# Adding the expert sums into the residual: products with gate 2 before the last expert's values, and the residual store on another queue

## The chip, the cores and the metric

The kernel runs on one core of a Trainium2 chip. The metric is the device time of one execution in microseconds (us). A core has five engines that run side by side, each from its own queue in order: TensorE (PE in the profile, PEld its weight loads), VectorE (DVE), ScalarE (ACT), GpSimd (POOL) and SyncE (SP, which here only issues DMAs). Matrix products land in PSUM; VectorE and ScalarE read it, GpSimd does not.

## The reference

Two layers work on 256 tokens `x` and 256 context tokens `xc`, each 1024 wide, in float32. In each layer:

```
mod        = silu(c) @ w_ada + b_ada          # six parts of 1024: ..., gt2
x          = x + gt1 * (mixers(norm(x), norm(xc)) @ w_out)
x          = x + gt2 * moe(norm(x))           # 16 experts, 2 of them per token
xc         = the same with its own gates, in the first layer only
```

`moe` sums, per token, gate times expert output. The final output is `rms_norm(x)` times a gain. The change touches only how `x + gt2 * moe` (and `xc + gtc2 * moe`) is put together, and what follows it.

## The kernel before, in words

**Experts.** `moe` runs 16 steps one after the other. Each step gathers the rows of one expert, multiplies them by w1, w3 and w2 (six weight blocks of 1 MB, loaded by SP), and adds its rows, scaled by the routing gate, to a table `ybd` in device memory by an accumulating DMA from GpSimd (`add_rows`). The first layer has four row tiles of 128 (two of context, two of tokens), the second has two.

**The last step.** Step 15 does not go through memory. `expert32(..., last=True)` takes its 64 rows in two halves n of 512 columns: TensorE's product stands in PSUM in two groups of 64 partitions, which ScalarE copies and VectorE adds (`s`). In the first layer ScalarE then makes the high part `yh` (gate times value, rounded for the fast matmul) and VectorE the low part `yl`. In the second layer VectorE first multiplies by the routing gate and by gate 2 (`SCALAR_TENSOR_TENSOR`), ScalarE rounds it to `yh`, VectorE subtracts to get `yl`. One-hot matrices `ohT`, made by VectorE, put the 64 rows at their tokens in a matmul.

**Combining.** `combine_g2` loads gate 2, broadcast to 128 partitions (two rows in the first layer: context and tokens). `combine_rows` loads the other steps' sums from `ybd` into `yr`; in the second layer GpSimd multiplies them by gate 2. `combine` then makes, per row tile and half, one PSUM sum of three products: identity times `yr` (float32), `ohT` times `yh`, `ohT` times `yl`. In the first layer VectorE multiplies that sum by gate 2 and adds it to the residual `x2` (GpSimd does two of the eight additions); in the second layer it adds it at once. The token tiles of the first layer are stored to `x1d` by SP.

**Into the second layer.** `ln1` squares `x2` on ScalarE, makes the reciprocal root on VectorE (`ssa`, then `lnms` to `lnz`), scales (`xs`), and TensorE transposes (`tp`). The first four half blocks of `w_in` are split into `hi` (ScalarE) and `lo` (VectorE) for the first matmuls (`early`). SP streams `w_in` blocks (w) and `w_ada` blocks (a, for the modulation of the same layer) through a ring of three 1 MB buffers, in a list made by `stream`; a block's load can start when the block three places ahead of it has been used. With `EARLY = 3` three a blocks stand behind the first two w blocks and are multiplied (`ada_next`) ahead of the transposes; the other thirteen are spread between the ten later w blocks. Their matmuls are then called from the mixer's matmul loop (`gemm`).

**Order.** Semaphores, buffers and the order in each engine's queue are set when the program is built: of the instructions that a time estimate holds for ready, the one written first goes first, so that a later one can fill a gap. `issue_after(i)` puts what its block writes on i's engine behind i. The mixer's steps are interleaved by a list scheduler with an estimate of its own (`Clocks`). In the profile every instruction has one line, L382, that of a helper; tiles tell them apart: `raw` is any of the weight ring's tiles, among them `yr`, gate 2, `yh` and `yl`; `yf` holds `x2`, and `s` the scratch of the last step.

Of the kernel before, what the change touches and what calls it, by code (L numbers as in the profile page):

```python
# [10 lines left out]
F32 = mybir.dt.float32  # L11
# [5 lines left out]
ALU = mybir.AluOpType  # L17
# [27 lines left out]
ADA_SLACK = (-1.0, 1.0)  # L45
PR = (60, 60)
LATE = 0
EARLY = 3
GH = (1, 3)
KORD = ((4, 5, 6, 7, 2, 3, 0, 1), (0, 1, 6, 7, 4, 5, 2, 3))  # L50
SLOTS = (32, 32)
NPRE = 3
# [336 lines left out]
class Kern:  # L389
# [478 lines left out]
    def ln1(self, l, xt):  # L868

        nc = self.nc  # L870
        ssq = self.s([P, 4, 2], "ssq")
        xs = []
        for i in range(4):
            t = self.pg("xs", D)
            for n in range(2):
                nc.scalar.activation(t[:, n * 512:n * 512 + 512], xt[i][n], AF.Square, accum_out=ssq[:, i, n:n + 1])
            xs.append(t)
            if l == 0 and i % 2 or i == 3:
                i0 = i - 1 if l == 0 else 0
                n = i + 1 - i0  # L880
                q = self.s([P, n], "ssa")
                nc.vector.tensor_tensor(q, ssq[:, i0:i + 1, 0], ssq[:, i0:i + 1, 1], op=ALU.add)
                r = self.rstd(q, n, D, "ln")
                for j in range(n):
                    nc.vector.tensor_scalar(xs[i0 + j][:, 0:512], xt[i0 + j][0], r[:, j:j + 1], None, op0=ALU.mult)
                    nc.scalar.activation(xs[i0 + j][:, 512:1024], xt[i0 + j][1], AF.Copy, scale=r[:, j:j + 1])

        self.hhi, self.hlo, self.early = [], [], []
        blocks = ORDER[l][0] + ORDER[l][1]
        parts = []  # L890
        for j in range(4):
            parts.append(self.split(self.take("w", l, j // 2)[:, j % 2 * 1024:(j % 2 + 1) * 1024]))
            if j % 2:
                self.used("w", l, j // 2)

        def early(k):
            if k == 0:
                for j in range(4):
                    ps = self.psmm() if j < 2 else self.pssc()
                    t = slice(256 if l == 1 and blocks[j][0] in XONLY else 0, 512)  # L900
                    self.early.append((ps, t))
            for j, (ps, t) in enumerate(self.early):
                hi, lo = parts[j]
                c = slice(k * P, k * P + P)
                self.mm3(ps[:, t], hi[:, c], lo[:, c], self.hhi[k][:, t], self.hlo[k][:, t], k == 0, k == KB - 1)

        for _ in range(l * EARLY):
            self.ada_next()
        for k in range(KB):
            pt = self.pstp()  # L910
            for i in range(4):
                nc.tensor.transpose(pt[:, i * P:(i + 1) * P], xs[i][:, k * P:(k + 1) * P], self.ident)
            if l == 0:
                self.ada_next()
            if k:
                early(k - 1)
            if l == 0:
                self.ada_next()
                if k == 3:
                    self.loads2()  # L920
            full = self.pg("full", 512)
            for c in range(2):
                sl = slice(256, 512) if c == 0 else slice(0, 256)
                nc.scalar.activation(full[:, sl], pt[:, sl], AF.Identity, bias=self.mc[l, 0][:, k, c:c + 1],
                                     scale=self.mc[l, 1][:, k, c:c + 1])
            hi, lo = self.hilo()
            self.splitx(hi, lo, full, "dve")
            self.hhi.append(hi)
            self.hlo.append(lo)
        early(KB - 1)  # L930
# [987 lines left out]
    def moe(self, l, route):  # L1918
# [29 lines left out]
        for e in range(NE):  # L1948
            if e == STAT:

                while len(self.pre) < AHEAD2[l]:
                    m, j = USE[self.wi]
                    self.pre.append(self.fetch(source(m)(j)))
                self.extras(l)
            if STAT <= e + 2 < NE:
                for n in both(e + 2):
                    xg[n] = self.gather(l, *sl[n], m=min(P, SLOT[l][e + 2]))
            for j in range(2):
                if e or j:
                    next(gens[e])  # L1960
                if e:
                    next(gens[e - 1], None)
            next(gens[e])
            if e:
                next(gens[e - 1], None)
            if e == NE - 1:
                while self.wi < len(USE):
                    self.pre.append(self.fetch(source(USE[self.wi][0])(USE[self.wi][1])))
                self.combine_g2(l)
            if e + 1 < NE:  # L1970
                begin(e + 1)
            next(gens[e])
        for _ in gens[NE - 1]:
            pass
        with tc.issue_after(self.last_y.ins):
            self.combine_rows(l)
        self.gate_open += 1
        self.pump()
        with tc.issue_after(self.last_y.ins), tc.issue_after(self.last_mm.ins):
            self.combine(l)  # L1980

    def yring(self):
# [9 lines left out]
    def combine_g2(self, l):  # L1992
        t = self.ring_tile()
        self.g2r = {}
        for c in ((1, 0) if l == 0 else (0,)):
            self.g2r[c] = t[:, c]
            self.nc.sync.dma_start(t[:, c], self.modd[l][c:c + 1, 5 * D:6 * D].to_broadcast([P, D]))
        if l == 1:
            fg = self.I["fg"]
            self.fgr = t[:, 1]  # L2000
            self.nc.sync.dma_start(self.fgr, bass.AP(tensor=fg.tensor, offset=fg.offset, ap=[[0, P], [1, D]]))

    def combine_rows(self, l):

        nc = self.nc
        ot = self.otiles(l)
        self.yr = {}
        for a in range(0, len(ot), 2):
            t = self.ring_tile()
            for j in range(2):  # L2010
                self.yr[ot[a + j]] = t[:, j]
                nc.sync.dma_start(t[:, j], self.ybd[l][(a + j) * P:(a + j + 1) * P])
        if l == 1:
            for i in ot:
                y = self.yr[i]
                nc.gpsimd.tensor_tensor(y, y, self.g2r[0], op=ALU.mult)

    def wdyn(self, l, i):

# [131 lines left out]
    def expert32(self, l, wsrc, tile, m, last=False):  # L2151
# [76 lines left out]
        for n in range(2):  # L2228
# [5 lines left out]
            if G > 1:  # L2234
# [2 lines left out]
                nc.scalar.copy(t, py[m:2 * m])  # L2237
                nc.vector.tensor_tensor(t, t, ps, op=ALU.add)
                ps = t
            if last and l == 1:  # L2240
                yf = self.pg("s1", 512)[:m]
                nc.vector.scalar_tensor_tensor(yf, ps, g, self.g2r[0][:m, c], op0=ALU.mult, op1=ALU.mult)
                nc.scalar.copy(yh[:, c], yf)
                self.last_y = nc.vector.tensor_tensor(yl[:, c], yf, yh.bitcast(F32)[:, c], op=ALU.subtract)
            elif last:
                nc.scalar.activation(yh[:, c], ps, AF.Copy, scale=g)
                self.last_y = nc.vector.scalar_tensor_tensor(yl[:, c], ps, g, yh.bitcast(F32)[:, c], op0=ALU.mult, op1=ALU.subtract)
            else:
                nc.scalar.activation(y[:m, c], ps, AF.Copy, scale=g)
        if not last:  # L2250
# [2 lines left out]
    def combine(self, l):  # L2253

        nc = self.nc
        yh, yl = self.ylast
        ot = self.otiles(l)
        col = lambda h: slice(h * 512, h * 512 + 512)

        def rows(a, h, ps):  # L2260
            nc.tensor.matmul(ps, lhsT=self.ident, rhs=self.yr[ot[a]][:, col(h)], start=True, stop=False)
            return ps

        def last(a, h, ps):
            nc.tensor.matmul(ps, lhsT=self.ohT[:, a], rhs=yh[:, col(h)], start=False, stop=False)
            nc.tensor.matmul(ps, lhsT=self.ohT[:, a], rhs=yl[:, col(h)], start=False, stop=True)
            return self.x2[ot[a]][h]

        if l == 1:
            for a in range(2):  # L2270
                ps = [rows(a, h, self.psmm() if a + h == 2 else self.pssc()) for h in range(2)]
                for h in range(2):
                    x = last(a, h, ps[h])
                    nc.vector.tensor_tensor(x, x, ps[h], op=ALU.add)
            return
        for u, (a, h) in enumerate((a, h) for a in range(len(ot)) for h in range(2)):
            i = ot[a]
            ps = rows(a, h, self.psmm() if u % 2 == 0 else self.pssc())
            x = last(a, h, ps)
            t = self.pg("s1", 512)  # L2280
            nc.vector.tensor_tensor(t, ps, self.g2r[1 if i < 2 else 0][:, col(h)], op=ALU.mult)
            (nc.gpsimd if u in GH else nc.vector).tensor_tensor(x, x, t, op=ALU.add)
            if i >= 2:
                nc.sync.dma_start(self.x1d[(i - 2) * P:(i - 1) * P, col(h)], x)

    def final(self, xt):
        nc = self.nc
# [74 lines left out]
```

## Time and profile before

| | us |
|---|---|
| median of 3 runs (1287.60, 1287.61, 1290.16) | 1287.61 |
| the profiled execution | 1286.5 |
| its span, first to last instruction | 1283.3 |
| busy TensorE / VectorE / ScalarE / GpSimd | 1135.7 / 723.3 / 531.7 / 162.0 |
| mean granted clock of TensorE | 0.941 |

The span is 3.2 us shorter than the execution. The first layer's combine lies at 709 to 727 us of the span, the second layer's at 1262 to 1273. A row of a timeline gives start, duration, engine, operation, output and inputs, size, number of instructions merged, and in brackets the engine's idle time before it with what ended it. A clock of 1.00 is 2.4 GHz, one of 0.50 is 1.2 GHz.

### The profile page before, as it was taken

The page shows a single profiled execution, that of the slowest core. Times are in us where ns is not written, and L with a number is a line of the kernel's source. Part 1 is how long each engine was busy: PE and PEld are TensorE (multiplying, and loading weights), DVE is VectorE, ACT ScalarE, POOL GpSimd, SP SyncE. Part 2 cuts the span into 40 slices and gives each one's busy share as a digit, 9 for nine tenths or more (in the row PEclk, how much of TensorE's full clock was granted, in tenths as well). Part 3 has the DMA queues.
Part 4 walks back from the last instruction along what each step waited for, and adds up shares of the span by engine and source line. Part 5 has one row for each costly group of instructions (what it writes and reads, how often), then busy time and mean ns, then how long its engine had stood idle before and what let it go on. Part 6 is the DMA issues. An engine that isn't in the chain of part 4 may idle for free. (4 is left out here: it accounts for less than half of the span.)

```text
span 1283.3 us, 16883 instructions
## 1 busy us (share of the span) xinstructions
PE 1135.7 (88%) x5789; PEld 717.1 (56%) x5789; DVE 723.3 (56%) x1824; ACT 531.7 (41%) x877; POOL 162.0 (13%) x204
## 2 busy tenths in 40 slices
PE   4999999997968699999998799998893699998885
PEld 2677677765856566655444277684671353533331
DVE  6496579788588464554544659599975010101115
ACT  5222642675326454555434452553940122212222
POOL 0200200100003210211100100100102111111012
PEclk9999999997988799999999899998995899999997
DMA  8763752544918698899995744554467899999971
GB/s 315 260 232 130 253 213 91 184 159 153 364 66 314 242 337 326 306 371 383 385 376 167 278 176 126 198 179 164 143 245 310 318 344 386 369 382 397 402 301 67
DMA packets 62011, 334.06 MB, mean 260 GB/s; under 512 B 12218, under 2 KB 13658, under 8 KB 27105
## 3 DMA queue, kind: packets, MB, share of 16 engines
q1 hardware_dynamic: 51840, 313.44, 64.3%
q0 software_dynamic: 10080, 19.50, 5.9%
q8 instruction: 47, 0.77, 0.2%
q14 instruction: 44, 0.35, 0.1%
HBM read 317.51 MB, written 19.15 MB: 262 GB/s over the span
## 5 line engine op out<-in xcount | busy, mean ns | idle before, releaser
L382 DVE TENSOR_TENSOR lo<-raw,hi 128x1024 fp32r<-128x1024 f32 x172 | 206.6, 1221 | 85.7 <-ACT hi L382 80.1
L382 ACT CAST hi<-raw 128x1024 fp32r<-128x1024 f32 x169 | 172.2, 1047 | 112.6 <-PE mm L382 52.9
L382 PE MATMUL sc<-raw,ah 128*64 128x512 f32 (+3 forms) x750 | 213.3, 628 | 6.2 <-SPq L2030 3.8
L382 PEld LDWEIGHTS sc<-raw,ah 128*64 128x64 f32 (+3 forms) x750 | 61.4, 145 | 105.0 <-issue 92.5
L382 PE MATMUL mm<-hi,ah 128*128 128x512 f32 (+3 forms) x264 | 108.7, 413 | 4.8 <-ACT hi L382 4.6
L382 PE MATMUL mm<-lo,ah 128*128 128x512 f32 (+3 forms) x264 | 106.7, 404 | 1.7 <-DVE lo L382 1.6
L382 PE MATMUL mm<-hi,al 128*128 128x512 f32 (+3 forms) x264 | 105.7, 402 | 0.7 <-DVE al L382 0.6
L382 PE MATMUL mm<-raw,ah 128*64 128x512 f32 (+3 forms) x378 | 102.1, 606 | 1.9 <-DVE rel L382 1.9
L382 DVE COPY al<-sc 128x512 f32<-128x512 f32 x21 | 14.5, 691 | 133.0 <-PE sc L382 133.0
L382 PE MATMUL mm<-ah,hi 128*128 128x512 f32 (+1 forms) x224 | 86.5, 391 | 1.2 <-DVE ah L382 1.2
L382 PE MATMUL mm<-ah,lo 128*128 128x512 f32 (+1 forms) x224 | 83.1, 372 | 0.9 <-DVE lo L382 0.9
L382 PE MATMUL mm<-al,hi 128*128 128x512 f32 (+1 forms) x224 | 82.9, 370 | 0.0
L382 PE MATMUL sc<-hi,ah 128*128 128x512 f32 (+3 forms) x176 | 74.8, 426 | 5.8 <-ACT hi L382 3.7
L382 PE MATMUL ad<-raw,cT 128*32 128x256 f32 (+1 forms) x512 | 67.6, 524 | 10.7 <-DMA raw<-in_wada_dram 9.1
L382 DVE TENSOR_TENSOR s<-s,mm 64x512 f32<-64x512 f32 (+1 forms) x43 | 29.2, 679 | 83.7 <-ACT s L382 83.7
L382 PE MATMUL sc<-lo,ah 128*128 128x512 f32 (+3 forms) x176 | 72.7, 413 | 1.6 <-DVE lo L382 1.6
L382 PE MATMUL sc<-hi,al 128*128 128x512 f32 (+3 forms) x176 | 72.3, 411 | 1.9 <-DVE al L382 1.9
L382 PEld LDWEIGHTS mm<-raw,ah 128*64 128x64 f32 (+3 forms) x378 | 33.1, 145 | 59.8 <-issue 53.0
L382 PEld LDWEIGHTS mm<-hi,ah 128*128 128x128 f32 (+3 forms) x264 | 49.3, 187 | 29.0 <-ACT hi L382 6.5
L382 PEld LDWEIGHTS tp<-fold,al 128*128 128x128 f32 x336 | 42.1, 198 | 40.2 <-ACT al L382 15.6
L382 PE MATMUL tp<-cst,xg 64*128 64x64 f32 (+4 forms) x264 | 31.4, 261 | 32.9 <-DMA xg<-h2d,rtab 14.3
L382 PE MATMUL tp<-fold,al 128*128 128x64 f32 x336 | 45.9, 286 | 16.0 <-ACT al L382 8.6
(433 smaller groups left out, 1977.0 us busy)
## 6 DMA issues: line engine op xcount, KB each, us to landing
raw<-in_wmoe_dram SPq DMA_DIRECT2D x192, 1024.0 KB
raw<-in_wada_dram SPq DMA_DIRECT2D x32, 1024.0 KB
raw<-in_win_dram SPq DMA_DIRECT2D x24, 1024.0 KB
raw<-in_wad_dram SPq DMA_DIRECT2D x16, 1024.0 KB
raw<-in_wout_dram SPq DMA_DIRECT2D x8, 1024.0 KB
x<-in_tok_dram SPq DMA_DIRECT2D x8, 512.0 KB
raw<-ybd SPq DMA_DIRECT2D x6, 512.0 KB
slot<-yf SPq DMA_DIRECT2D x36, 64.0 KB
```

The source lines that it names most:

```text
L382: r = f(*a, **k)
```

## The change

Gate 2 is multiplied into the last step's values in both layers. In the first layer a step's rows can be context or tokens, so `slot_gains` makes one gain row per slot on VectorE: a 0/1 column `late` from the row numbers, the difference of the two gate rows, and one fused multiply and add; the instructions of the stage after it are written behind it on VectorE. The sums of the other steps are multiplied by gate 2 and added to `x2` without TensorE: in the first layer tile 0 on VectorE, tiles 2 and 3 on GpSimd, and tile 1 is multiplied on GpSimd but still added by the identity product; in the second layer tile 2 is multiplied on GpSimd and added on VectorE, tile 3 all on GpSimd. `combine_rows` and `combine` are no longer written behind the last `yl`. `combine` goes half by half over the tiles and adds each PSUM sum to `x2` on VectorE. The `x1d` stores are issued by ScalarE. `EARLY` is 1, and in the second layer the four `lo` of the first `w_in` blocks are written behind the last `xs` of VectorE.

```diff
-EARLY = 3
-GH = (1, 3)
+EARLY = 1
...
-                    nc.vector.tensor_scalar(xs[i0 + j][:, 0:512], xt[i0 + j][0], r[:, j:j + 1], None, op0=ALU.mult)
+                    xi = nc.vector.tensor_scalar(xs[i0 + j][:, 0:512], xt[i0 + j][0], r[:, j:j + 1], None, op0=ALU.mult)
...
-        for j in range(4):
-            parts.append(self.split(self.take("w", l, j // 2)[:, j % 2 * 1024:(j % 2 + 1) * 1024]))
-            if j % 2:
-                self.used("w", l, j // 2)
+        with self.tc.issue_after(xi.ins) if l == 1 else ExitStack():
+            for j in range(4):
+                parts.append(self.split(self.take("w", l, j // 2)[:, j % 2 * 1024:(j % 2 + 1) * 1024]))
+                if j % 2:
+                    self.used("w", l, j // 2)
...
                 self.combine_g2(l)
-            if e + 1 < NE:
-                begin(e + 1)
+                with tc.issue_after(self.slot_gains(l, sl[e][0], SLOT[l][e])):
+                    next(gens[e])
+                continue
+            begin(e + 1)
             next(gens[e])
         for _ in gens[NE - 1]:
             pass
-        with tc.issue_after(self.last_y.ins):
-            self.combine_rows(l)
+        self.combine_rows(l)
         self.gate_open += 1
         self.pump()
-        with tc.issue_after(self.last_y.ins), tc.issue_after(self.last_mm.ins):
+        with tc.issue_after(self.last_mm.ins):
             self.combine(l)
...
+    def slot_gains(self, l, rows, m):
+        nc = self.nc
+        last = next(i for i in reversed(nc.obj.cur_bb.bb.instructions) if i.engine == mybir.EngineType.DVE)
+        if l == 1:
+            return last
+        late = self.s([P, 1], "late", bufs=1)[:m]
+        with self.tc.issue_after(last):
+            nc.vector.tensor_scalar(late, rows[:m], 255.5, None, op0=ALU.is_gt)
+        t = self.pg("raw3", 2048)
+        d, self.g2s = t[:m, 0:D], t[:, D:2 * D]
+        nc.vector.tensor_tensor(d, self.g2r[0][:m], self.g2r[1][:m], op=ALU.subtract)
+        i = nc.vector.scalar_tensor_tensor(self.g2s[:m], d, late, self.g2r[1][:m], op0=ALU.mult, op1=ALU.add)
+        return i.ins
...
-        if l == 1:
-            for i in ot:
-                y = self.yr[i]
-                nc.gpsimd.tensor_tensor(y, y, self.g2r[0], op=ALU.mult)
+        tt = lambda e, *a, **k: (nc.gpsimd if e else nc.vector).tensor_tensor(*a, **k)
+
+        for i, (mul, add) in zip(ot, ((0, 0), (1, 2), (1, 1), (1, 1)) if l == 0 else ((1, 0), (1, 1))):
+            y = self.yr[i]
+            tt(mul, y, y, self.g2r[1 if l == 0 and i < 2 else 0], op=ALU.mult)
+            for h in range(2) if add < 2 else ():
+                tt(add, self.x2[i][h], self.x2[i][h], y[:, h * 512:h * 512 + 512], op=ALU.add)
...
-            if last and l == 1:
+            if last:
                 yf = self.pg("s1", 512)[:m]
-                nc.vector.scalar_tensor_tensor(yf, ps, g, self.g2r[0][:m, c], op0=ALU.mult, op1=ALU.mult)
+                nc.vector.scalar_tensor_tensor(yf, ps, g, self.g2s[:m, c], op0=ALU.mult, op1=ALU.mult)
...
-            elif last:
-                nc.scalar.activation(yh[:, c], ps, AF.Copy, scale=g)
-                self.last_y = nc.vector.scalar_tensor_tensor(yl[:, c], ps, g, yh.bitcast(F32)[:, c], op0=ALU.mult, op1=ALU.subtract)
...
-        for u, (a, h) in enumerate((a, h) for a in range(len(ot)) for h in range(2)):
-            i = ot[a]
-            ps = rows(a, h, self.psmm() if u % 2 == 0 else self.pssc())
-            x = last(a, h, ps)
-            t = self.pg("s1", 512)
-            nc.vector.tensor_tensor(t, ps, self.g2r[1 if i < 2 else 0][:, col(h)], op=ALU.mult)
-            (nc.gpsimd if u in GH else nc.vector).tensor_tensor(x, x, t, op=ALU.add)
-            if i >= 2:
-                nc.sync.dma_start(self.x1d[(i - 2) * P:(i - 1) * P, col(h)], x)
+        tiles = (1, 0, 2, 3) if l == 0 else (0, 1)
+        for u, (h, a) in enumerate((h, a) for h in range(2) for a in tiles):
+            i = ot[a]
+            ps = self.psmm() if u % 2 == 0 else self.pssc()
+            if l == 0 and a == 1:
+                nc.tensor.matmul(ps, lhsT=self.ident, rhs=self.yr[i][:, col(h)], start=True, stop=False)
+            nc.tensor.matmul(ps, lhsT=self.ohT[:, a], rhs=yh[:, col(h)], start=l == 1 or a != 1, stop=False)
+            nc.tensor.matmul(ps, lhsT=self.ohT[:, a], rhs=yl[:, col(h)], start=False, stop=True)
+            x = self.x2[i][h]
+            nc.vector.tensor_tensor(x, x, ps, op=ALU.add)
+            if l == 0 and i >= 2:
+                nc.scalar.dma_start(self.x1d[(i - 2) * P:(i - 1) * P, col(h)], x)
```

## Rows read from the trace of the kernel before

**Rows 1.** Windows: length; busy of PE, PEld, DVE, ACT, POOL; PEclk; DMA; GB/s

```profile
728.00:738.00 10.00, 5.61 (x24) 1.83 (x24) 4.92 (x19) 3.02 (x5) 1.36 (x3) 0.50 0.97 358
...
760.00:870.00 110.00, 109.26 (x632) 83.03 (x631) 90.71 (x246) 53.52 (x89) 8.63 (x20) 1.00 0.51 173
...
870.00:890.00 20.00, 16.14 (x67) 7.04 (x66) 17.52 (x73) 2.48 (x4) 0.00 (x0) 0.83 0.50 175
...
920.00:930.00 10.00, 6.21 (x40) 5.22 (x39) 10.00 (x49) 9.82 (x21) 2.18 (x6) 0.80 0.31 108
```

**Rows 2.** Timeline, first layer: last expert step and residual (columns: start, us, engine ...)

```profile
702.12 1.75 SPq L382 DMA_DIRECT2D raw<-ybd  x4
...
702.81 0.69 DVE L382 COPY al<-sc 128x512 f32<-128x512 f32 x1 [8.69 <-PE sc L382]
...
705.63 0.66 DVE L382 TENSOR_SCALAR ah<-iota_b,rel 64x128 fp32r<-64x128 bf16 x3
...
708.18 0.68 DVE L382 TENSOR_TENSOR s<-s,mm 64x512 f32<-64x512 f32 x1 [1.51 <-ACT s L382]
...
709.17 1.13 PE L382 MATMUL mm<-raw,cst 128*128 128x512 f32 x2
...
711.78 0.74 DVE L382 SCALAR_TENSOR_TENSOR raw<-s,rtab,raw 64x512 fp32r<-64x512 f32 x1 [0.79 <-ACT raw L382]
```

**Rows 3.** Timeline, first layer: GpSimd beside VectorE while the residual is added

```profile
714.54 1.27 POOL L382 TENSOR_TENSOR yf<-yf,s 128x512 f32<-128x512 f32 x1 [15.86 <-DVE s L382]
...
715.56 0.80 DVE L382 TENSOR_TENSOR yf<-yf,s 128x512 f32<-128x512 f32 x1
```

**Rows 4.** Timeline, layer boundary: residual end, norm chain, first matmuls of layer two

```profile
716.27 1.99 ACT L382 CAST hi<-raw 128x1024 fp32r<-128x1024 f32 x2 [1.30 <-DMA raw<-in_win_dram]
...
723.29 1.07 PE L382 MATMUL ad<-raw,cT 128*32 128x512 f32 x8
...
725.76 0.69 DVE L382 TENSOR_TENSOR yf<-yf,s 128x512 f32<-128x512 f32 x1
...
726.36 2.35 DVE L382 TENSOR_TENSOR lo<-raw,hi 128x1024 fp32r<-128x1024 f32 x2
...
728.63 0.16 DVE L382 TENSOR_TENSOR ssa<-ssq 128x4 f32<-128x4 f32 x1
...
731.66 1.68 DVE L382 TENSOR_SCALAR xs<-yf,lnz 128x512 f32<-128x512 f32 x4
...
735.16 1.93 PE L382 MATMUL ad<-raw,cT 128*32 128x512 f32 x8 [0.31 <-DMA raw<-in_wada_dram]
...
737.02 1.33 PE L382 MATMUL tp<-cst,xs 128*128 128x128 f32 x5
...
739.07 0.73 PE L382 MATMUL mm<-ah,hi 128*128 128x512 f32 x2
```

**Rows 5.** Timeline, end of the second layer: row products, last step, norm

```profile
1252.64 0.80 SPq L382 DMA_DIRECT2D raw<-ybd  x2
...
1256.29 4.65 POOL L382 TENSOR_TENSOR raw<-raw,raw 128x1024 f32<-128x1024 f32 x2 [5.77 <-PE tp L382]
...
1257.05 3.97 DVE L382 TENSOR_SCALAR ah<-iota_b,rel 64x128 fp32r<-64x128 bf16 x2
...
1262.08 0.74 DVE L382 SCALAR_TENSOR_TENSOR s<-s,rtab,raw 64x512 f32<-64x512 f32 x1
...
1266.25 0.68 DVE L382 TENSOR_TENSOR raw<-s,raw 64x512 fp32r<-64x512 f32 x1 [0.68 <-ACT raw L382]
...
1272.35 0.68 DVE L382 TENSOR_TENSOR yf<-yf,mm 128x512 f32<-128x512 f32 x1
...
1273.83 0.71 DVE L382 TENSOR_TENSOR ssa<-ssq 128x2 f32<-128x2 f32 x1 [0.80 <-ACT xs L382]
```

**Rows 6.** Window: the clock while the second layer's last w2 product runs

```profile
1256.00:1262.00 6.00, 5.07 (x17) 1.46 (x16) 5.12 (x6) 0.96 (x2) 4.65 (x2) 0.72 0.10 42
```

**Rows 7.** Timeline, TensorE in the second mixer: a modulation product after its load

```profile
882.43 1.91 PE L382 MATMUL ad<-raw,cT 128*32 128x512 f32 x2 [1.06 <-DMA raw<-in_wada_dram]
```

More of the change, by code (lines that the diff above doesn't have):

```diff
@@ L1997, in combine_g2 @@
             self.nc.sync.dma_start(t[:, c], self.modd[l][c:c + 1, 5 * D:6 * D].to_broadcast([P, D]))
+        self.g2s = self.g2r[0]
         if l == 1:
@@ L2258, in combine @@
         col = lambda h: slice(h * 512, h * 512 + 512)
[L2260 to L2265, printed above, removed]
-            nc.tensor.matmul(ps, lhsT=self.ohT[:, a], rhs=yl[:, col(h)], start=False, stop=True)
[L2267 to L2275, printed above, removed]
-        for u, (a, h) in enumerate((a, h) for a in range(len(ot)) for h in range(2)):
-            i = ot[a]
-            ps = rows(a, h, self.psmm() if u % 2 == 0 else self.pssc())
-            x = last(a, h, ps)
-            t = self.pg("s1", 512)
-            nc.vector.tensor_tensor(t, ps, self.g2r[1 if i < 2 else 0][:, col(h)], op=ALU.mult)
-            (nc.gpsimd if u in GH else nc.vector).tensor_tensor(x, x, t, op=ALU.add)
-            if i >= 2:
-                nc.sync.dma_start(self.x1d[(i - 2) * P:(i - 1) * P, col(h)], x)
+        tiles = (1, 0, 2, 3) if l == 0 else (0, 1)
[5 more added lines that the diff above has]
+            nc.tensor.matmul(ps, lhsT=self.ohT[:, a], rhs=yh[:, col(h)], start=l == 1 or a != 1, stop=False)
+            nc.tensor.matmul(ps, lhsT=self.ohT[:, a], rhs=yl[:, col(h)], start=False, stop=True)
+            x = self.x2[i][h]
+            nc.vector.tensor_tensor(x, x, ps, op=ALU.add)
+            if l == 0 and i >= 2:
+                nc.scalar.dma_start(self.x1d[(i - 2) * P:(i - 1) * P, col(h)], x)
     def final(self, xt):
```

## The prediction

> **What bounds the kernel now.** I read the shares of the engines first (TensorE is busy 88% of the span), then the timelines of the two places that the change touches, then windows over what follows. In both places no engine is full: the time is a chain of short steps. In the first layer VectorE adds the last pair of halves at 726.45, the norm's sum `ssa` starts at 728.63, the scaling `xs` at 731.66, and the first main matmul of layer two at 739.07 [rows 4]. `ssa` was not late because of the squares but because two `lo` (2.35 us) stood in front of it until 728.71; and the transposes ended late because a modulation product (`ad`, 1.93 us) stood in front of them, waiting for its load [rows 4]. In the second layer the last addition ends at 1273.03, `ssa` follows at 1273.83, and the rest to the end is not touched [rows 5]. After the boundary the mixer keeps TensorE at 109.26 of 110 us, with two thin stretches (16.14 of 20, 6.21 of 10) in which VectorE is full (17.52 of 20, 10.00 of 10) [rows 1]. No later stage starts at a fixed time, so a shift at the boundary is carried to the end.
>
> **First layer: the sums of the other steps.** Their loads are issued at 702.12, as before [rows 2]. In the second layer the first use came 3.65 us after the issue (1252.64 to 1256.29) [rows 5]; so the first tile is there at about 705.8, and at 358 GB/s [rows 1] each further 0.52 MB takes 1.46 us: 707.2, 708.7, 710.2 (estimates). VectorE has its one-hot rows done by 706.7 (0.66 us from 705.63 and one more) [rows 2] and can take tile 0's product, 1.18 us (half of the 2.35 for two of 128x1024) [rows 4], until 707.9. GpSimd has three products at 2.33 us (4.65 for two [rows 5]) and four additions at 1.27 [rows 3]: 12.1 us, all reading SBUF.
>
> What decides is whether VectorE can work beside them. Where GpSimd's two products ran, VectorE's two one-hot instructions took 3.97 us [rows 5] against 0.66 for three [rows 2]; they ended with GpSimd's (1261.02, 1260.94). `ssa`, two SBUF inputs, took 0.71 against 0.16 beside another GpSimd product [rows 4, 5]. So a VectorE instruction of this kind waits until GpSimd's present one is over. On the row nearest in shape, an addition of 512 columns from two SBUF tiles, 0.80 us was spent against the usual 0.69 [rows 3, 4]; by that alone the price would be 0.1 us each. It began 0.25 us before GpSimd's end, so it could not show more, and I take the full wait. The Trainium skill, "SBUF — State Buffer", section "Who interferes with whom", says that a VectorE instruction with two SBUF inputs contends with a GpSimd one that reads SBUF, and that the later fully blocks. By the 0.1 us reading the sum is that of the first rival below, by the rule that of the forecast.
>
> From 707.9 GpSimd and VectorE then take turns. Up to the second `yl` VectorE has six instructions with two SBUF inputs (tile 0's two additions at 0.69, two fused products at 0.74, two `yl` at 0.68: 4.2 us), GpSimd six (three products and three additions: 10.8): 722.9, less small overlaps 722.6. Before, `yl` ended at 712.52 [rows 2]. The residual additions from PSUM (0.69, one SBUF input) need no turn; eight of them, one put into a wait: 4.8 us more, last addition at about 727.5 instead of 726.45: +1.0. The eight identity products on TensorE (1.13 us the pair [rows 2]) become two and give nothing back, since VectorE is now last. Bounds of the last addition: 720 (no waiting) and 729.5 (tile 0's work behind the last step's).
>
> The square and its read follow as in the second layer, 0.80 us [rows 5], behind the issue of the last store: four issues took 1.75 us on SP [rows 2], so at most 0.44; I take 0.3. `ssa` starts at 728.6, as before: what the `lo` gave back is spent. The stores now wait for their additions in ScalarE's queue; behind them stand only the squares, which wait for the same additions. On SP the next `a` and w loads no longer queue behind the stores; instead w0's and w1's buffers come free later, after the `lo` (about 735 and 737), while the 96 products of the four early half blocks still lie ahead: nothing on the path.
>
> From `ssa` on: 3.03 us of chain and 1.68 of `xs` [rows 4], then the four `lo` that now stand behind, 4 x 1.18 = 4.7, and a first cast of about 0.5: 9.9 us to the first main matmul, against 10.44 before. The transposes (1.33 for five) and ScalarE's work fit beside the `lo`. Gain 0.5.
>
> **The clock and the moved blocks.** Before, the granted clock was 0.50 from 728 to 738, while TensorE had little to do, and the two `ad` blocks ran at that rate (1.93 against 1.07 us) [rows 1, 4]; it was back before the main matmuls. Now there is nothing between the transposes and those matmuls, so I expect these to begin at half clock. The nearest price is the end of layer two: mean 0.72 over 6 us, so 0.28 x 6 / 0.5 = 3.4 us at half [rows 6]; half of it is lost, +1.7. Bounds 0 and 5 (ten us at half [rows 1]). Two `ad` blocks of 1.07 us move into the mixer: 2.1 if TensorE is the limit there, 0 if they fall into the 7.7 us of the thin stretches; +1.1.
>
> The gain rows (a subtraction and a fused step of 1024 columns, about 2.6 us) lie ahead of VectorE's copy at 702.81, in front of which it was idle 8.69 us [rows 2]: nothing, at worst 1 us if gate 2 lands late, since the copy stands behind them and the fold products wait for it.
>
> Sum of the first layer: +1.0 - 1.0 (`lo` out of the way, less the store's issue) - 0.5 + 1.7 + 1.1 = +2.3.
>
> **Second layer.** GpSimd's two products end at 1260.94 [rows 5]; its two additions now follow, to 1263.5 if alone. The first fused product, 1262.08 before, waits until 1262.2 and ends at 1262.95; then GpSimd's second addition, until 1264.2; a row addition 0.69, `yl` 0.68, `s` 0.68, the fused product 0.74, another row addition 0.69 and `yl`: 1268.6 against 1266.93 [rows 5], +1.7. Behind it stood 6.10 us (to 1273.03: two additions, four float32 identity products at half clock, two additions); now four additions of 0.67: 1271.3. Gain 1.7. `ssa` no longer meets GpSimd, 0.55 less. Sum -2.3; bounds 0 (both row additions in front of `s`) and -4 (no waiting).
>
> **Total: +2.3 - 2.3 = 0.** The profiled execution took 1286.5, 1.1 below the median of the runs (0.09%); between the two I predict 1287.0.
>
> **Rivals.**
> 1. GpSimd and VectorE do not hold each other up, or the order keeps them apart. For it: the 0.80 row. Then `yl` ends at about 714, the additions with GpSimd at 719 to 721; ScalarE is last: its casts of `w_in` end at 718.26 [rows 4], eight squares of 0.63 and four issues: 724.5, `ssa` 4.0 earlier. First layer -4.0 - 0.5 + 2.8 = -1.7, second -3.9: 1281.4.
> 2. Slower: the ring. With two `a` blocks ahead, a w block's load waited in two of ten places for the w block before it (w6, w9); with `EARLY = 1` it does in w4, w6, w8 and w10, besides w2. A load issued only after the split lands 3.65 + 2.9 us later. Where TensorE's remaining products are shorter than that, it stands, and the mixer gets another thin stretch: 3.9 us, as from 870 to 890 [rows 1], where a product already waited for its load [rows 7]. Against it: the blocks before hold mostly more work. 1287.0 + 3.9 = 1290.9.
> 3. The clock is up in time and the moved blocks fall into idle time: 1287.0 - 2.8 = 1284.2. For it: 7.7 us of idle TensorE; against: ten us at 0.50 [rows 1].
>
> **How the numbers follow.** A measurement tells 0.2%, 2.6 us. Forecast 0.39 (its own range 1284 to 1290: faster 0.06, same 0.26, slower 0.07), first rival 0.28 (faster 0.27), second 0.24 (slower 0.20, same 0.04), third 0.09 (faster 0.07, same 0.02); the rest of the first is same. Faster 0.40, same 0.33, slower 0.27. Range 1280.5 to 1292: it takes in most of both outer rivals and the bound of the clock.
>
> **What would show it.** Right: fused products and `yl` of the first layer at 1 to 3 us each with ends at those of GpSimd, second `yl` near 722, `ssa` near 728.6, PEclk 0.5 in the first main matmuls, last addition of layer two about 1.7 us earlier. Wrong: `yl` by 716 (first rival), a w load for which TensorE waits (second), full clock at the first main matmul (third).

## The result: 0.73% slower, and the profile after

| | before | after |
|---|---|---|
| median of 4 runs, us | 1288.82 | 1299.57 |
| profiled execution and its span, us | 1286.5, 1283.3 | 1301.45, 1299.8 |
| granted clock, mean | 0.941 | 0.927 |

The ratio is 1.0073, 95% interval 1.0049 to 1.0096. The prediction was 1287.0 us, range 1280.5 to 1292: too low, and on the wrong side.

Up to the last step of the first layer both programs have the same instructions in every queue, apart from the gain rows; the profiled execution of after is 3.9 us later there. Each stretch below is read from one profiled execution of either kernel, by starts unless an end is named:

| stretch, us | before | after |
|---|---|---|
| copy `al<-sc` of the last step to second `yl` (end) | 9.72 | 11.76 |
| ... to the last addition (end) | 23.64 | 28.55 |
| ... to `ssa` | 25.83 | 30.93 |
| ... to the first main matmul of layer two | 36.26 | 40.39 |
| first main matmul to the router's first product, the mixer | 217.31 | 226.43 |
| router's product to the first gathered rows' transposes | 29.35 | 30.98 |
| from there to the second layer's `ssa` | 288.10 | 285.96 |

So 4.1 us are lost at the boundary and 9.1 in the mixer behind it, and 2.1 are gained at the second layer's end. The router's 1.6 can't be told from the spread: over all the kernels of this document that stretch takes 29.0 to 33.2 us, with the change or without. The last stretch holds the second layer's experts too, which take 265.5 to 272.3 us in kernels where nothing touches them; that the gain is at its end is read further down. Lost and gained together make 11.1, and the medians differ by 10.75; with one execution each, so close an agreement is partly luck.

The boundary in the timeline of after; the rows answer to [rows 2 to 4]:

```profile
706.72 0.69 DVE L381 COPY al<-sc 128x512 f32<-128x512 f32 x1 [0.16 <-PE sc L381]
...
713.20 0.33 SPq L381 DMA_DIRECT2D raw<-in_wada_dram  x1
...
713.63 2.13 SPq L381 DMA_DIRECT2D raw<-ybd  x4
...
716.37 0.74 DVE L381 SCALAR_TENSOR_TENSOR s<-s,rtab,raw 64x512 f32<-64x512 f32 x1
...
717.79 0.68 DVE L381 TENSOR_TENSOR raw<-s,raw 64x512 fp32r<-64x512 f32 x1 [0.68 <-ACT raw L381]
...
722.27 4.64 POOL L381 TENSOR_TENSOR raw<-raw,raw 128x1024 f32<-128x1024 f32 x2 [19.67 <-DMA raw<-ybd]
...
724.67 2.08 PE L381 MATMUL mm<-raw,cst 128*128 128x512 f32 x2 [3.48 <-POOL raw L381]
...
732.79 0.69 DVE L381 TENSOR_TENSOR yf<-yf,mm 128x512 f32<-128x512 f32 x1 [3.25 <-PE mm L381]
...
734.11 1.52 ACTq L381 DMA_DIRECT2D x1d<-yf  x3
734.59 0.68 DVE L381 TENSOR_TENSOR yf<-yf,sc 128x512 f32<-128x512 f32 x1
...
735.67 0.63 ACT L381 ACTIVATE xs<-yf 128x512 f32<-128x512 f32 x1 [1.44 <-DVE yf L381]
...
737.65 0.16 DVE L381 TENSOR_TENSOR ssa<-ssq 128x4 f32<-128x4 f32 x1 [2.38 <-ACT xs L381]
...
747.11 1.22 PE L381 MATMUL mm<-ah,hi 128*128 128x512 f32 x2 [0.86 <-DVE ah L381]
```

The loads of the row sums are issued at 713.63, behind that of `a0`, whose buffer came free only at 713.20; before, they were issued 0.69 us ahead of the copy [rows 2]. The last step's chain ends at 718.47, with fused products of 0.74 us and `yl` of 0.68, so GpSimd did not hold it up: it starts only at 722.27. TensorE then waits for GpSimd's product and runs at half clock (2.08 us for the identity pair, 1.13 before [rows 2]), and VectorE waits for TensorE. Three stores then stand in front of the last squares, so `ssa` follows the last addition by 2.4 us. The first main matmuls take 0.61 us each, at half clock, against 0.37 [rows 4].

The mixer as one window (columns as in [rows 1]), first of before, then of after:

```profile
739.07:956.38 217.31, 208.32 (x1147) 155.96 (x1145) 173.33 (x502) 110.29 (x189) 17.18 (x41) 0.97 0.48 168
...
920.00:935.00 15.00, 11.21 (x69) 9.19 (x68) 13.93 (x57) 10.43 (x22) 2.18 (x6) 0.77 0.42 142
```

```profile
747.11:752.50 5.39, 5.39 (x14) 4.39 (x15) 3.63 (x7) 1.93 (x4) 0.00 (x0) 0.51 1.00 410
...
925.00:957.00 32.00, 26.16 (x143) 20.99 (x143) 25.98 (x85) 24.26 (x46) 5.53 (x13) 0.84 0.22 76
...
747.11:973.54 226.43, 215.54 (x1157) 159.67 (x1158) 177.35 (x502) 114.15 (x191) 16.30 (x40) 0.95 0.47 164
```

TensorE stands 10.9 us in place of 9.0, and is busy 7.2 us longer. Two modulation blocks are 2.1 of that; the start at 0.51 is 0.49 x 5.39 = 2.6. Nearly all of the rest lies in the thin stretch at 925 to 957: TensorE is idle for 5.8 us there, against 3.8 in the one of before at 920 to 935, and if its busy time is weighted with the clock granted at each moment, 4.7 us are lost to the half clock, against 2.6. Who ends TensorE's waits in the mixer (line waited for, us in total, times, longest), first before, then after:

```profile
PE mm L382 <- ACT hi L382: 3.2, 1, 3.2
PE sc L382 <- DVE Q L382: 2.8, 3, 1.1
PE ad L382 <- DMA raw<-in_wada_dram: 1.1, 1, 1.1
```

```profile
PE sc L381 <- DVE Q L381: 4.1, 5, 1.0
PE sc L381 <- ACT yf L381: 1.8, 1, 1.8
PE tp L381 <- DVE yf L381: 1.6, 2, 0.9
PE mm L381 <- ACT yf L381: 1.3, 2, 0.9
```

No product of after's mixer waits for a load itself; the waits are for the short steps of VectorE and ScalarE, more and in other places than before. ScalarE did wait for loads, from the same window:

```profile
ACT hi L381 <- DMA raw<-in_win_dram: 11.7, 4, 9.6
```

Before, it was 1.0 in all. The 9.6 us end at 887.48, and little of them reached TensorE: the next product that waited for a `lo` stood 0.37 us, and behind its casts ScalarE waited another 13.0 us for a product of TensorE.

The second layer's end, after [rows 5]:

```profile
1275.05 4.66 POOL L381 TENSOR_TENSOR raw<-raw,raw 128x1024 f32<-128x1024 f32 x2 [5.78 <-PE tp L381]
...
1279.79 2.93 POOL L381 TENSOR_TENSOR yf<-yf,raw 128x512 f32<-128x512 f32 x2
1280.43 1.17 DVE L381 SCALAR_TENSOR_TENSOR s<-s,rtab,raw 64x512 f32<-64x512 f32 x1
...
1285.33 0.68 DVE L381 TENSOR_TENSOR raw<-s,raw 64x512 fp32r<-64x512 f32 x1 [0.68 <-ACT raw L381]
1285.94 1.28 DVE L381 TENSOR_TENSOR yf<-yf,raw 128x512 f32<-128x512 f32 x2
...
1288.34 1.27 DVE L381 TENSOR_TENSOR yf<-yf,sc 128x512 f32<-128x512 f32 x2
...
1290.48 0.71 DVE L381 TENSOR_TENSOR ssa<-ssq 128x2 f32<-128x2 f32 x1 [0.87 <-ACT xs L381]
```

From GpSimd's products to `ssa` it is 15.43 us, before 17.54. All eight kernels of this document with the changed second layer take 15.43 or 15.44 there, the eleven others 17.1 to 18.3, so this gain of some 2 us is shown.

### The profile page after: what moved, and what is told of

It reads as the page before. It is cut to its first block, busy times and chain, and to the rows that moved or that the text cites. A ratio compares the mean times of both kernels' runs of the same rounds, so it can differ in the third digit from the quotient of the medians.

```text
span 1299.8 us, 16856 instructions
## 1 busy us (share of the span) xinstructions
PE 1139.6 (88%) x5769; PEld 724.2 (56%) x5769; DVE 731.0 (56%) x1828; ACT 537.0 (41%) x881; POOL 173.9 (13%) x211
## 3 DMA queue, kind: packets, MB, share of 16 engines
q10 hardware_dynamic: 576, 1.05, 0.2%
```

## The experiments

Ratios are to the kernel before, run in turn on the same chip, with 95% intervals; "boundary" is copy to first main matmul, "mixer" as in the table, both from one profiled execution.

**1. The parts of the change.** Four kernels: the row loads back in front; EARLY back at 3; EARLY and `lo` alone; the second layer alone.

```diff
 # rows_first = after, with
-        self.pump()
+        with tc.issue_after(self.yrd.ins):      # the last load of row sums
+            self.pump()
 # after_early3 = after, with
-EARLY = 1
+EARLY = 3
 # before_early1 = before, with
-EARLY = 3
+EARLY = 1
+        with self.tc.issue_after(xi.ins) if l == 1 else ExitStack():   # the four splits
 # before_layer2 = before, with the changed combine for l == 1 only
```

> The changed kernel, but the loads of the summed rows stand in SyncE's queue ahead of w0, w1 and a0 of layer two again. Queue theory: in the changed kernel these loads were issued at 713.63 behind a0's wait for its buffer, some 7.5 us later than their place before, and that delay is most of what was lost at the boundary; here the first use of the rows comes 6 to 8 us earlier and the norm's sum ssa 4 to 5 us earlier, so about 1295 us, 0.45% over the kernel before. Rival, the lock: VectorE and GpSimd hold each other up in any case, so an earlier landing only moves the contention in front of the last step's yl; ssa moves by under 1.5 us and the time stays at 1298 to 1299.

> The changed kernel with three modulation blocks ahead of the mixer of layer two (EARLY = 3) in place of one. The mixer's instructions then stand in the order of the kernel before. Order theory: about 5 to 8 us of the loss lie in that mixer, whose order the one constant rearranged; so 1292 us, 0.25% over the kernel before. Rival: the mixer lost its time because it started late and at half clock, whatever its order; then 1298 to 1300, as the changed kernel.

> The kernel before with EARLY = 1 and the four lo behind xs, and nothing else of the change. Order theory: 5 to 8 us slower in the mixer, about 1295 us, 0.5% over the kernel before, and that without any change to the combine. Rival: the constant costs nothing by itself, 1288 to 1290.

> The kernel before with the second layer's part of the change alone: the other steps' rows are added to the residual by VectorE and GpSimd, and the identity products are gone. By the changed kernel's profile the stretch from the last step's first one-hot rows to ssa shrank from 16.8 to 14.7 us, so 1286.7 us, 0.16% under the kernel before. Rival: part of that shortening was TensorE's clock in that one execution, and under 1 us is left.

| kernel | ratio | boundary | mixer |
|---|---|---|---|
| rows_first | 1.0073 (1.0047 to 1.0098) | 38.87 | 225.3 |
| after_early3 | 0.9998 (0.9980 to 1.0017) | 40.53 | 216.7 |
| before_early1 | 1.0065 (1.0040 to 1.0090) | 33.41 | 226.5 |
| before_layer2 | 0.9978 (0.9954 to 1.0003) | 37.80 | 216.5 |

EARLY = 1 with the `lo` behind `xs` brings nearly the whole loss without any change to the combine, and with EARLY back at 3 the rest of the change comes out even. The late loads were not it: in front again, they bring the last addition from 28.55 to 26.69 and `ssa` from 30.93 to 29.68 only, and the time shows nothing (its interval is 0.25% to either side). The queue theory falls for the time. The second layer's part alone is a gain of 2.8 us by the runs; its interval just touches 1. Its boundary is that of before and yet takes 37.80 us in place of 36.26, so single executions differ by 1.5 there.

**2. EARLY and `lo` taken apart, the clock, the stores.**

```diff
 # lo_behind = before + the splits behind xs;  early1_only = before + EARLY = 1
 # warm = before_early1, ahead of the transposes:
+            for n in range(20):
+                tensor.matmul(ps[32 * j:32 * j + 32, :], lhsT=self.cT[:, 0, :], rhs=xt[3][1], ...)
 # stores_sync = after_early3, with
-                nc.scalar.dma_start(self.x1d[...], x)
+                nc.sync.dma_start(self.x1d[...], x)
```

> The kernel before with the four lo of the early half blocks queued behind xs on VectorE, and EARLY left at 3; the mixer keeps its order. Both theories on EARLY expect this half of the edit to be harmless: ssa 1.8 us earlier, the transposes no earlier than the modulation block in front of them lets them, 1289 us, ratio 0.998 to 1.001. A rival: it is this half that costs the 8 us (the early half blocks wait for lo), then 1295 or more.

> The kernel before with EARLY = 1 and the lo left where they were. Theory: the constant costs by itself, through the half clock at the first main matmuls (2 to 3 us), the two blocks moved into the mixer (2.1) and its new order (2 to 3); 1295 to 1298 us. Rival: the constant and the lo cost only together; then 1289 to 1291.

> The kernel before with EARLY = 1 and the lo behind xs, and 20 more products of a modulation block's shape on TensorE, ahead of the transposes of layer two, from the residual just added; their result is not used. Clock theory: in the kernel without them the first main matmuls ran at 0.50 for 5 us because TensorE had stood for 6 us before the transposes; with them the clock is up at the first main matmul and 2 to 3 us come back, 1296 to 1297 us. Rival: the clock there is not what costs; the same 1299 as without them.

> The changed kernel with EARLY = 3, and the four stores of the residual issued by SyncE again. Queue theory: on ScalarE three of them stood 1.52 us in front of the last squares, so ssa comes 1.5 us earlier against the last addition and the time is 1 to 1.5 us under that of the kernel with EARLY = 3 (ratio to the kernel before 0.9988). Rival: the modulation block in front of the transposes, which waits for its load, sets their start, and nothing is gained (ratio 0.9998).

| kernel | ratio | boundary | mixer |
|---|---|---|---|
| lo_behind | 0.9992 (0.9969 to 1.0015) | 33.92 | 217.4 |
| early1_only | 1.0025 (1.0005 to 1.0044) | 34.88 | 221.6 |
| warm | 1.0046 (1.0022 to 1.0070) | 33.42 | 223.5 |
| stores_sync | 0.9988 (0.9968 to 1.0007) | 39.12 | 215.4 |

The `lo` behind `xs` gain 2.3 us at the boundary (`ssa` 3.0 earlier), which the time doesn't show. The constant costs alone, but 3 us and not 8. Warming TensorE took 3.0 us off the mixer's stretch, as the clock theory said; the intervals of the two ratios overlap, so in the time it is not shown. With SyncE storing, `ssa` follows the last addition by 0.84 us in place of 2.38; in the time this is not shown either.

**3. The boundary without the mixer, and the mixer without the boundary.**

```diff
 # blocks_later = lo_behind, with one block ahead and, in the loop over k:
+            if l == 1 and k in (1, 2):
+                with self.tc.issue_after(self.last_mm.ins):
+                    self.ada_next()
 # slack = before, with
-ADA_SLACK = (-1.0, 1.0)
+ADA_SLACK = (-1.0, 3.0)
 # early2 = lo_behind with EARLY = 2;  layer2_lo = before_layer2 + lo_behind
```

> The kernel before with the lo behind xs, EARLY left at 3 and the loads and the mixer in their old order, but the products of the second and third modulation block forced behind the first half block's main matmuls. So it has what EARLY = 1 does at the boundary (half clock at the first main matmuls, two blocks no longer in front of them), and not its mixer. Order theory: half clock 2 to 3 us, blocks 1 to 2, less the 1.8 us that the transposes come earlier: 1292 us, ratio 1.001 to 1.003. Rival, the boundary is the whole loss: 1297 to 1299, ratio 1.006.

> The kernel before with the planner's allowance for a modulation block's load in layer two raised from 1 to 3 us (ADA_SLACK). The boundary is the same; the mixer's instructions are arranged anew, with the same work. Order theory: the stretch from the first main matmul of layer two to the first gathered rows' transposes, 246 to 249 us in all kernels with the old order, changes by 2 us or more, and the time with it, whichever way. Rival: TensorE has the same work, the order costs nothing; 1289 to 1291 us, the stretch within 246 to 249.

> The kernel before with EARLY = 2 and the lo behind xs. If each block that leaves the boundary had its price (4 us each by the 8.4 of two), the time is 1294 to 1295 us. Order theory: another arrangement of the mixer, so anything from 1289 to 1298 us, and the sign is read from the stretch between the first main matmul and the first gathered rows' transposes, with its waits and its half clock.

> The two parts of the change that did not cost, together: the kernel before with the second layer's combine of the change and the lo behind xs in front of layer two; EARLY 3, the first layer's combine as before. If the two add up, ratio 0.997 (1287 us). Rival: the lo's part is spent on waiting for the modulation block in front of the transposes; ratio 0.998, as the second layer's part alone.

| kernel | ratio | boundary | mixer |
|---|---|---|---|
| blocks_later | 1.0001 (0.9985 to 1.0017) | 33.43 | 221.6 |
| slack | 1.0085 (1.0063 to 1.0107) | 36.47 | 230.0 |
| early2 | 1.0008 (0.9982 to 1.0035) | 33.93 | 220.6 |
| layer2_lo | 0.9939 (0.9912 to 0.9967) | 33.94 | 217.0 |

Main matmuls of blocks_later and the first of the two blocks behind them, by its timeline:

```profile
735.67 1.22 PE L382 MATMUL mm<-ah,hi 128*128 128x512 f32 x2 [0.86 <-DVE ah L382]
...
740.45 1.57 PE L382 MATMUL ad<-raw,cT 128*32 128x512 f32 x8
...
742.29 0.39 PE L382 MATMUL mm<-al,hi 128*128 128x512 f32 x1
```

It has the half clock at the first matmuls (0.61 us, then 0.39) and both blocks on TensorE's path. Its mixer is 4.3 us longer than that of before, its boundary 2.8 shorter, and it comes out even. So the half clock and the blocks, which EARLY = 1 brings at the boundary, are some 4.3 us of the 9.1 that the mixer lost; the other 4.9 are its new arrangement (226.5 in before_early1, whose mixer has the order of after in every queue). These parts are good to 2 or 3 us: the eight kernels with EARLY = 3 and the mixer's order of before take 215.4 to 220.8 us there, those with the order of after and no warming 225.3 to 226.5. In the time, blocks_later and before_early1 differ clear of noise.

That an arrangement alone can cost is shown by slack: it has the boundary of before and the same work, and loses 11 us. Its waits in the mixer:

```profile
PE tp L382 <- DVE yf L382: 6.8, 2, 6.1
PE sc L382 <- ACT yf L382: 5.3, 1, 5.3
PE tp L382 <- DVE slot L382: 3.3, 3, 2.8
```

The constant also changed slack's loads, and ScalarE waited 19.7 us in all for those of `w_in`; so "arrangement" means the order of the instructions together with that of the loads, and no run takes the two apart. early2 comes out even, with a mixer of 220.6, 3.2 us over that of lo_behind; whether one block has the price of 4 us that its expectation names, its interval doesn't settle. layer2_lo is faster than both kernels, by 0.61% against before.

**4. Is it the constant, or the arrangement it happened to get?** And the first layer without the mixer.

```diff
 # early1_slack0, 2, 3 = before_early1, with the second value
-ADA_SLACK = (-1.0, 1.0)
+ADA_SLACK = (-1.0, 0.0)      # 2.0, 3.0
 # rows_stores = rows_first with EARLY = 3 and the stores on SyncE
 # no_gpsimd = rows_stores, GpSimd's row work of the first layer left out
+            if l == 0 and mul:
+                continue
```

> The kernel before with EARLY = 1 and the lo behind xs, and the planner's allowance for a modulation block's load at 0 in place of 1 us: the same work in another arrangement. Arrangement theory: the mixer's stretch, 226 us without it, comes out anywhere between 221 and 232, and the time follows it. Rival, the constant is bad by itself: 225 to 227 again, 1298 to 1300 us.

> As the one before, with the allowance at 2 us. Arrangement theory: a third arrangement, a third time, 221 to 232 us in the mixer. Rival: 225 to 227.

> As the one before, with the allowance at 3 us, the value that cost 11 us with EARLY = 3. Arrangement theory: the value has no fixed price, so it may be better than the 226 us of EARLY = 1 alone. Rival, the value is bad by itself as EARLY = 1 is: 226 plus 10.

> The changed kernel with EARLY = 3, the loads of the row sums in front of w0, w1 and a0, and the stores on SyncE. By the kernels with one of the two: from the last step's copy of its sums to the last addition 26.7 us (23.64 before, 28.4 with the loads behind), to ssa 27.5 (25.83 before), to the first main matmul 37 to 38 (36.26 before, 39.1 with the loads behind). Theory that GpSimd beside VectorE and the products at half clock keep the rest: it stays 3 us over the last addition of before, and the kernel is at 0.998 of the kernel before. Rival, the loads were the whole loss: last addition at 23 to 24 and ratio 0.995.

> The kernel with the row loads in front, the stores on SyncE and EARLY = 3, and GpSimd's three products and four additions of the first layer left out (so the residual lacks the other steps' rows of three tiles). Lock theory: with GpSimd silent the fused products and yl take their 0.74 and 0.68 us, and the second yl ends 9.7 us after the copy of the last step's sums, or 10.9 if VectorE's own product (1.2 us) stands in front of it, in place of 14.75; the last addition at 22 to 23 us in place of 26.8. Rival, VectorE's own queue is what is late: the second yl stays at 13 to 15.

| kernel | ratio | boundary | mixer |
|---|---|---|---|
| early1_slack0 | 1.0073 (1.0049 to 1.0096) | 33.40 | 225.2 |
| early1_slack2 | 1.0058 (1.0029 to 1.0088) | 33.42 | 227.3 |
| early1_slack3 | 1.0047 (1.0021 to 1.0073) | 34.69 | 223.9 |
| rows_stores | 0.9996 (0.9978 to 1.0014) | 37.73 | 219.3 |
| no_gpsimd | one run: 1290.52 us, before 1289.52 | 31.64 | 220.8 |

None of the first three comes near 221: four arrangements with EARLY = 1 and the `lo` behind take 223.9 to 227.3 us. That speaks for the constant being bad together with this placing of `lo`; the value 3 has no fixed price either, being the best here and costing 11 us with EARLY = 3.

In rows_stores the second `yl` ends 14.75 us after the copy and the last addition 26.77, as expected. GpSimd and VectorE of rows_stores, then VectorE of no_gpsimd, whose residual lacks the other steps' rows of three tiles:

```profile
710.27 5.11 POOL L381 TENSOR_TENSOR raw<-raw,raw 128x1024 f32<-128x1024 f32 x2 [8.72 <-DMA raw<-ybd]
...
711.76 1.41 DVE L381 SCALAR_TENSOR_TENSOR s<-s,rtab,raw 64x512 f32<-64x512 f32 x1
713.85 2.07 DVE L381 TENSOR_TENSOR raw<-s,raw 64x512 fp32r<-64x512 f32 x1 [0.68 <-ACT raw L381]
715.45 4.41 POOL L381 TENSOR_TENSOR yf<-yf,raw 128x512 f32<-128x512 f32 x2
...
716.56 1.05 DVE L381 SCALAR_TENSOR_TENSOR s<-s,rtab,raw 64x512 f32<-64x512 f32 x1
...
718.67 1.74 DVE L381 TENSOR_TENSOR raw<-s,raw 64x512 fp32r<-64x512 f32 x1
720.34 4.50 DVE L381 TENSOR_TENSOR yf<-yf,raw 128x512 f32<-128x512 f32 x2
724.77 1.27 DVE L381 TENSOR_TENSOR yf<-yf,sc 128x512 f32<-128x512 f32 x2
```

```profile
716.52 0.74 DVE L381 SCALAR_TENSOR_TENSOR s<-s,rtab,raw 64x512 f32<-64x512 f32 x1
717.95 0.68 DVE L381 TENSOR_TENSOR raw<-s,raw 64x512 fp32r<-64x512 f32 x1 [0.68 <-ACT raw L381]
...
722.46 1.28 DVE L381 TENSOR_TENSOR yf<-yf,raw 128x512 f32<-128x512 f32 x2
...
725.92 1.28 DVE L381 TENSOR_TENSOR yf<-yf,sc 128x512 f32<-128x512 f32 x2
```

Without GpSimd's work the last addition ends 21.42 us after the copy, 5.3 sooner and ahead of before (23.64): the lock theory's 22 to 23, a little better. VectorE's steps with two SBUF inputs are short again, but not all of the 5.3 need be that: the additions of tiles 2 and 3 no longer have to wait for GpSimd's results either. The second `yl` ends at 13.09, the rival's figure: VectorE's own product and an addition had moved in front of it. The boundary is 4.6 us shorter than before and the mixer 3.5 longer, and of the time one run each tells nothing.

## Why the prediction was wrong, point by point

| term of the sum, us | forecast | measured |
|---|---|---|
| last addition of the first layer | +1.0 | +4.9 |
| from it to `ssa` (`lo` away, stores on ScalarE) | -1.0 | +0.2 |
| `ssa` to the first main matmul | -0.5 | -1.0 |
| half clock at the first main matmuls | +1.7 | +2.6 |
| two blocks in the mixer | +1.1 | +2.1 |
| the rest of the mixer | no term | +4.4 |
| second layer | -2.3 | -2.1 |

- **The step that failed.** "Two `ad` blocks of 1.07 us move into the mixer: ... +1.1" took the mixer's order as given. Two list schedulers make that order from time estimates, and the constant also changes the stream of loads they see. The mixer took 9.1 us more, of which 2.1 are the blocks in full, 2.6 the half clock at its start, and 4.4 a new arrangement (4.9 by blocks_later): more waits for VectorE and ScalarE, and the half clock that goes with them. That the arrangement costs is shown by before_early1 against blocks_later; why this one does is only read from its waits.
- **A second step failed.** The last addition of the first layer, "+1.0", was +4.9, and +6.5 against kernels with the `lo` behind. The loads were not issued "as before" but behind w0, w1 and a0; with them in front, the last addition is still 3.1 late, and leaving GpSimd's row work out takes 5.3 away.
- **Half a step.** The taking of turns was not what happened in the changed kernel: the late loads kept GpSimd away until the last step's chain was over, and the sign "fused products and `yl` at 1 to 3 us" did not come. With the loads in front it came (1.05 to 2.07 us beside GpSimd, 0.74 and 0.68 without), so it was right in kind. But there the second `yl` was 5.0 us later than before, not the 10.1 worked out: GpSimd had done four instructions by then and not six, and VectorE's two additions came behind `yl`. Nor were all of the 5.0 turns: `yl` was 3.4 late in no_gpsimd and 2.0 in after, which leaves 1.7 to 3.0 for them.
- **A mis-sized term.** "I take 0.3" for the stores on ScalarE was about 1.5: three were issued in one go, 1.52 us, in front of the last squares.
- **Right.** The gain rows are hidden (0.16 us is left to TensorE in front of the copy), the half clock came, and the `lo` out of the way gave 3.0 at `ssa` in lo_behind, more than the 1.0 net of the text.
- **Right by luck.** The second layer: forecast -2.3, measured -2.1 in the trace and 0.22% (2.8) by runs. Its parts were off and made up for each other. The second `yl` came 0.3 later and not 1.7, since the row additions moved behind it; what follows to the last addition shrank by 2.5 and not 3.4; and the 0.55 at `ssa` did not come, since it still met GpSimd's last product (0.71 us), as before.
- **The rivals.** Slower was right with the second rival, its mechanism not: no product of the mixer waited for a w load, and of ScalarE's wait for one no more than some 0.4 us shows in TensorE's waits. The first rival's condition, that "the order keeps them apart", was met up to `yl`, by the late loads: with the 3.9 us of the later start taken off, the second `yl` ended at 714.6, the rival's "about 714". Its end was not: the last addition came at 731.4 on that scale, not at 719 to 721. That the two engines don't hold each other up at all is excluded by the stretched rows of rows_stores, and the third rival by the half clock.

What stays open: before_early1 and blocks_later differ by 0.64% (8 us) in the runs; their mixers differ by 4.9 in the trace, and where the remainder lies one execution of each doesn't tell. What in the arrangement costs, the instructions' order or the loads', was not taken apart. Nor was it settled whether some arrangement would make EARLY = 1 harmless; early1_only (221.6) came nearest.

## What to carry to other kernels

When the order of a stage is made by a planner, a small constant that moves two short blocks is a new order of the whole stage, and that can outweigh what was counted by hand: compare the stage's length, and lay the parts of a change on the chip one by one, since here 0.6% was to be gained in a change that lost 0.7%. Before work is given to GpSimd beside a chain on VectorE, allow for a stretch of each of the chain's steps with two SBUF inputs (0.3 to 1.4 us each here, beside GpSimd instructions of 1.3 to 2.3 us), and check by the order which of them really meet. A load that is written earlier isn't issued earlier: look at what the queue puts in front of it.

## What the runs showed of the hardware beyond what was expected

- The stretching works both ways: beside VectorE, GpSimd's two additions took 4.41 us in rows_stores, against 2.51 in after, where VectorE was mostly waiting; its two products took 5.11 against 4.64.
- VectorE's additions that read one input from PSUM are untouched: 1.27 us for two while GpSimd ran, 1.28 without it. The Trainium skill, "SBUF — State Buffer", section "Who interferes with whom", says that a VectorE instruction with at most one SBUF input, outside its two-port modes, does not contend with GpSimd; these rows agree.
- With the 20 unused products of 32x512 TensorE worked from 727.5 us on in warm, the clock stood at 1.00 from 732 on, and the main matmuls ran at full rate (0.37 us each for the first two); without them they ran at half clock for 5.5 us. The transposes began 1.6 us later for it, the main matmuls no later. The windows of warm, then that of before_early1 (columns as in [rows 1]):

```profile
732.00:738.87 6.87, 4.81 (x40) 2.17 (x32) 6.80 (x12) 4.49 (x8) 0.00 (x0) 1.00 0.93 315
738.87:745.00 6.13, 6.13 (x29) 5.07 (x30) 3.64 (x7) 1.93 (x4) 0.00 (x0) 1.00 0.96 351
```

```profile
737.49:743.00 5.51, 5.51 (x15) 4.47 (x16) 3.64 (x7) 1.93 (x4) 0.00 (x0) 0.51 0.99 402
```
